# Encoder layer: a plain half chunk behind the Strassen products, a written VectorE order, and x loaded again for the folded input

## The chip, the cores and the metric

The kernel runs on one core of one Trainium2 chip. The metric is the device time of one execution in microseconds; the median of several executions counts.

## The reference

All tensors are float32; the sequence has 1,024 positions, the model 1,024 columns.

```python
def reference(x, pre_g, post_g, w_in, ln_g, ln_b, w_s, b_s, w_f, b_f, w_out):
    h = rms_norm(x, pre_g)
    p = jnp.einsum('bsd,de->bse', h, w_in)
    u_a, v_a, g_a, z_b, g_b = jnp.split(p, 5, axis=-1)       # 512 columns each
    a = spatial_gating(gelu(u_a), gelu(v_a), w_s, b_s, ln_g, ln_b) * silu(g_a)
    b = fourier_mix(z_b, w_f, b_f) * silu(g_b)               # real part of a 2D DFT, then w_f
    y = jnp.einsum('bse,ed->bsd', jnp.concatenate([a, b], axis=-1), w_out)
    return x + rms_norm(y, post_g)
```

## The kernel before, in words

Every product is made in parts: an operand is split into a high part (fp32r, made by ScalarE in `split`, L71) and a low part (what is left, made by VectorE, L74), and `mm3` (L76) issues high times high, high times low and low times high. So a product of 128x128 by 128x512 is three instructions on TensorE, and nothing can be multiplied until ScalarE and VectorE have both handled it.

The program has four stages. **Start** (L82 to L156): eight blocks of x, transposed (`head` and `xr`), come in with the columns of `w_in` for v; ScalarE makes `hh`, VectorE `hl`, both scaled by `pre_g`, and TensorE starts with v for seven chunks of 128 positions. `vec_sb` holds `pre_g` and other vectors; `const_load` (L254) brings `w_f` and the tables, but the table `cs_sb` is loaded early on SP. **Features** (L423, `feature_tile`): twelve tiles of 128 features, each in two halves of 512 positions; the epilogue frees the bank `pf` with the VectorE operation `t<-pf,R` (L474, L481). Between them the function `after` (L493) places the other work by tables: the folded input of z (`z_fold`, L298, for eight blocks), the products with it (`z_step`), the gating heads and the DFTs. `z_fold` adds `hh` and `hl`, multiplies by `R` (the norm of each position), adds and subtracts mirrored positions into `sd`, and splits that into `fh` and `fl`. `feature_load` (L260) loads one tile's weights `wf` and splits them, `wz_load` (L225) loads z's weights and folds them into `fw`.

**Out projection** (L610 on). Eight chunks of 128 positions; chunk c has two halves n of 512 output columns. Chunks 0 and 1 are made plainly: four half chunks of two products each (L704), bank `py`. Chunks 2 to 7 are made in pairs g = 1, 2, 3 by seven Strassen products each, `q1` to `q7` and `p2` (a product is twelve instructions of 512 columns). Their weights are quarters of `w_out` (`11`, `12`, `21`, `22`) and sums of them, `T1` to `T4` (`w_sum`, L549): one part is added by VectorE, or by a load that accumulates on POOL's queue (L554), and the result is split again (`w_split`). `stream` (L687) makes the operands `cq` one step ahead. The results are combined on VectorE out of the banks `ba`, `bb`, `bc` into `y` (L744 to L775); `bb` is used by `q6`, then by `q7` and `q4`. `ORDER` (L601) runs group 1 by itself and interleaves groups 2 and 3; the last group's `q1` and `p2` are cut in two halves of 256 columns. `y_part` (L642) takes the sum of squares of a part: ScalarE squares, VectorE adds into `part`; `y_out` scales and stores: chunks below `DIRECT` (6) are scaled on VectorE (L667), get x by an accumulating load and go out; 6 and 7 have x loaded ahead.

All tiles of 4 KB a partition share 40 buffers (tag `S`); a tile waits for the last reader of its buffer. TensorE's order is the written one throughout; VectorE's is the written one from L729 on (`tc.manual_schedule`), and elsewhere, as on ScalarE, POOL and SP, a scheduler of the framework sets it when the program is built.

Of the kernel before, what the change touches and what calls it, by code (L numbers as in the profile page):

```python
# [8 lines left out]
F32 = mybir.dt.float32  # L9
# [5 lines left out]
P = 128  # L15
# [16 lines left out]
def encoder_layer_kernel(  # L32
# [48 lines left out]

    head = slot("head")  # L82
    wv0 = raw_slot("wv0")
    vec_sb = con.tile([P, 20], F32, name="vec_sb")
    nc.scalar.dma_start(vec_sb, x0[:, 0:20])
    nc.sync.dma_start(head[:, 0:256], x0[:, 20:276])
    nc.sync.dma_start(wv0[:, 0:512], w_nat[1, 0])
    nc.sync.dma_start(head[:, 256:1024], x0[:, 276:1044])
    pre_g, ln_g, b_f, ln_b = (vec_sb[:, a:b] for a, b in ((0, 8), (8, 12), (12, 16), (16, 20)))
# [28 lines left out]

    def square(kt):
        if kt == 0:  # L120
            nc.scalar.activation(sq, xs[kt], AF.Square)
        else:
            sq1 = tmp(f"sq{kt}")
            nc.scalar.activation(sq1, xs[kt], AF.Square)
            nc.vector.tensor_tensor(sq, sq, sq1, op=ALU.add)

    wvh = quad("wvh", (P, 8, 512), F32R)
    for kt in range(KT):
        if kt == 0:
# [12 lines left out]
        h = slot(f"hh{kt}", dt=F32R)  # L142
        l = slot(f"hl{kt}", dt=F32R)
        hh.append(h)
        hl.append(l)
        if kt == 0:
            split(wrv, wh, wl, hi_on_act=False)
        for sl in ([slice(0, 256), slice(256, 640), slice(640, 1024)] if kt == 0 else [slice(0, 1024)]):
            nc.scalar.activation(h[:, sl], xr[:, sl], AF.Copy, scale=pg)  # L149
            nc.vector.scalar_tensor_tensor(l[:, sl], xr[:, sl], pg, h[:, sl].bitcast(F32), op0=ALU.mult, op1=ALU.subtract)  # L150
        if kt > 0:
            split(wrv, wh, wl)
        if kt > 0:
            square(kt - 1)
        xs[kt] = xr
# [92 lines left out]

    wsTb = slot("wsTb", (P, 2, 512))
    ws_sb, Tb = wsTb[:, 0], wsTb[:, 1]  # L250
    cs_sb = con.tile([P, 129], F32, name="cs_sb")
    wf_sb = slot("wf_sb", (P, 512))

    def const_load():  # L254
        nc.sync.dma_start(ws_sb, w_sT)
# [41 lines left out]

    def z_fold(kt):  # L298
        hs = tmp(f"hs{kt}")
        nc.vector.tensor_tensor(hs, hh[kt].bitcast(F32), hl[kt].bitcast(F32), op=ALU.add)  # L300
        nc.vector.tensor_tensor(hs, hs, R, op=ALU.mult)
        sd = tmp(f"sd{kt}", (P, 2, 4, P))
        hv = hs.rearrange("p (b a) -> p a b", a=8)
        for i, op in enumerate((ALU.add, ALU.subtract)):
# [112 lines left out]

    wss = slot("wss", (P, 2, 512), F32R)
    split(ws_sb, wss[:, 0], wss[:, 1])
    wq.append(feature_load(1))  # L420


    def feature_tile(f, epilogue):  # L423
# [125 lines left out]
    def w_sum(key, i, base, add):  # L549
        t = raw.pop((base, i))  # L550
        if (add, i) in raw:
            nc.vector.tensor_tensor(t, t, raw[add, i], op=ALU.add)  # L552
        else:
            nc.gpsimd.dma_start(t, quarter(add, i), accum_op=ALU.add)  # L554
        raw[key, i] = t
        w_split(key, i, t)

    mixB = lambda: Bf[0]

# [38 lines left out]
        yield  # L598

    FULL = ("q1", "q5", "q6", "p2", "q7", "q3", "q4")  # L600
    ORDER = [(1, k) for k in FULL] + [(2, k) for k in ("q1", "q5", "q6", "q3", "q7")] + [(3, k) for k in FULL[:3]]  # L601
    ORDER += [(2, "q4"), (3, "q7"), (2, "p2")] + [(3, k) for k in ("q4", "q3", "p2")]
    WITH = {"q1": "11", "q5": "T1", "q6": "T2", "p2": "21", "q7": "T3", "q3": "22", "q4": "T4"}

    def product(o, t, key, start, stop, lo=0, hi=512):
# [4 lines left out]
    for f in range(8, 12):  # L610
        feature_tile(f, g_epilogue(lambda f=f: Bf[0][:, f - 8]))
        if f < 10:
            w_load(("11", "21")[f % 2], 0)
            del raw[("11", "21")[f % 2], 0]
        elif f == 10:
            for key in ("11", "21"):
                w_load(key, 1)
                del raw[key, 1]
        if f == 11:
            for key in ("12", "22"):  # L620
                for i in range(2):
                    w_raw(key, i)

    x_t = x.rearrange("(c p) d -> c p d", c=8)
    out_t = out.rearrange("(c p) d -> c p d", c=8)
    xin, yt, ssq, part = {}, {}, {}, {}
    pg_sb = slot("pg_sb")

    DIRECT = 6

    def x_load(c):
        if c < DIRECT:
            return
        xin[c] = slot(f"x{c}")
        nc.sync.dma_start(xin[c], x_t[c])
# [6 lines left out]
    def y_part(c, n, src, lo, hi, outs=()):  # L642
# [13 lines left out]
        if c >= DIRECT:  # L656
            nc.vector.tensor_tensor(yt[c][:, lo:hi], src, pg_sb[:, lo:hi], op=ALU.mult)  # L657
        if j == n - 1:
            if outs:
# [2 lines left out]
                due.append(c)  # L662

    def y_out(c, outs):
        if c < DIRECT:
            for src, lo, hi in ready[c]:
                nc.vector.scalar_tensor_tensor(yt[c][:, lo:hi], src, part[c], pg_sb[:, lo:hi], op0=ALU.mult, op1=ALU.mult)  # L667
            nc.gpsimd.dma_start(yt[c], x_t[c], accum_op=ALU.add)
        for lo, hi in outs:
            if c >= DIRECT:  # L670
# [6 lines left out]
    for key in ("12", "22"):  # L677
        for i in range(2):
            w_split(key, i, raw[key, i])
    for i in range(2):  # L680
        w_raw("11", i)
    nc.sync.dma_start(pg_sb, post_g.broadcast_to([P, D]))
# [4 lines left out]
    def stream():  # L687
        old = None
        for g, key in ORDER:
# [4 lines left out]
            old = o  # L694
            yield
        next(old)
        yield

    ahead = stream()
    def make_sum(j):  # L700
        for i in range(2):
            w_sum(sums[j][0], i, *sums[j][1:])

    for k in range(4):  # L704
        n, c = k // 2, k % 2
        if n == 0:
            yt[c] = slot(f"y{c}")
        py = bank(f"py{c}{n}")
        product(py, pl[c][0], "1" + str(n + 1), True, False)
        product(py, pl[c][1], "2" + str(n + 1), False, True)  # L710
        make_sum(k)
        next(ahead)
        if k == 1:
            for i in range(2):
                raw.pop(("22", i))
        if k > 1:
            next(ahead)
            x_load(c)
        y_part(c, 2, py, n * 512, n * 512 + 512, [(0, D)])

    lo, hi = slice(0, 512), slice(512, 1024)
    def y_due(cs):
        for c in list(cs):
            if c in due:
                due.remove(c)
                y_out(c, [(0, D)])

    at = {}
    ctx.enter_context(tc.manual_schedule(engines={mybir.EngineType.DVE}))  # L729
    for g, key in ORDER:  # L730
        a, b = 2 * g, 2 * g + 1
        last = g == 3
        op = ops.pop((g, key))
        before = due[:]
        if key == "q1":
            at[g] = [bank(f"b{n}{g}") for n in ("abcd" if last else "abc")]
            yt[a], yt[b] = slot(f"y{a}"), slot(f"y{b}")
        ba, bb, bc = at[g][:3]
        if key == "q1" and last:
            for t, (l, h) in zip((ba, at[g][3]), cuts):  # L740
                product(t[:, 0:256], op, "11", True, False, l, h)
                nc.scalar.copy(yt[b][:, l:h], t[:, 0:256])
        elif key == "q1":
            product(ba, op, "11", True, False)  # L744
            nc.scalar.copy(yt[b][:, lo], ba)
        elif key == "q5":
# [2 lines left out]
        elif key == "q6":  # L749
            product(bb, op, "T2", True, False)  # L750
            nc.vector.tensor_tensor(yt[a][:, hi], bb, yt[b][:, lo], op=ALU.subtract)
            x_load(b)
        elif key == "q7":
            product(bb, op, "T3", False, False)
            nc.vector.tensor_tensor(yt[b][:, hi], bb, yt[b][:, hi], op=ALU.add)
            y_part(b, 2, yt[b][:, hi], 512, 1024)
            x_load(a)
        elif key == "q4":
            product(bb, op, "T4", False, True)
            nc.vector.tensor_tensor(yt[b][:, lo], yt[b][:, lo], bb, op=ALU.subtract)  # L760
            y_part(b, 2, yt[b][:, lo], 0, 512)
        elif key == "q3":
            product(bc, op, "22", False, True)
            nc.vector.tensor_tensor(yt[a][:, hi], bc, yt[a][:, hi], op=ALU.add)  # L764
            if last:
                y_due(before)
            y_part(a, 3 if last else 2, yt[a][:, hi], 512, 1024)
        elif last:
            for t, (l, h) in zip((ba, at[g][3]), cuts):
                product(t[:, 0:256], op, "21", False, True, l, h)  # L770
                y_part(a, 3, t[:, 0:256], l, h, [(512, 1024), (0, 512)])
        else:
            product(ba, op, "21", False, True)
            y_part(a, 2, ba, 0, 512)
        y_due(before)  # L775
        next(ahead, None)
        if (g, key) == (2, "p2"):
            y_due(due)


def _dft_consts():
# [49 lines left out]
```

## Time and profile before

| what | value |
|---|---|
| median of 3 executions (lowest, highest) | 320.06 us (319.32, 320.10) |
| the profiled execution | 321.24 us |
| its span (first to last instruction) | 319.5 us |
| granted clock of TensorE, mean | 0.991 of full speed |
| busy: TensorE, VectorE, ScalarE, GpSimd | 96%, 78%, 42%, 8% |

The span is what the trace covers; the 1.7 us that the profiled execution takes beyond it are outside the program's instructions. The list of waits says for each engine what it waited for, by the instruction that released it. The timeline gives start and length of single instructions; the lengths of matrix products overlap, so the distance between two starts is what one costs.

### The profile page before, as it was taken

What the parts mean: (1) busy time and instruction counts of PE and PEld (TensorE: products, weight loads), DVE (VectorE), ACT (ScalarE), POOL (GpSimd) and SP (SyncE); (2) the same over time, 40 slices, a digit from 0 to 9 for tenths busy, and PEclk for the clock granted to TensorE, in tenths of its full rate; (3) what the DMA queues carried; (4) which work ended last, traced back from release to release, by engine and by line L of the source; (5) the groups of instructions that cost most, each with busy time, mean ns of one, the idle gap of its engine ahead of it and who ended that gap; (6) DMA issues with size and microseconds to landing.
All of it is one profiled execution on the core that took longest, in us unless ns stands there. A gap on an engine that the chain in (4) does not pass through costs nothing. (4 is left out here: it accounts for less than half of the span.)

```text
span 319.5 us, 4048 instructions
## 1 busy us (share of the span) xinstructions
PE 307.3 (96%) x1513; PEld 256.8 (80%) x1513; DVE 247.9 (78%) x465; ACT 134.0 (42%) x211; POOL 25.0 (8%) x35
## 2 busy tenths in 40 slices
PE   8999999999999999899999999999999999999990
PEld 7688888878888888788888888888888878888880
DVE  4599399899899899889746889663899887865562
ACT  4794467830311313342342343531746454333220
POOL 0000033200000000000000000000013420300140
PEclk9999999999999999999999999999999999999996
DMA  7984102021011120102010116730507855284067
GB/s 246 409 308 135 63 0 68 1 75 58 0 67 68 40 91 2 50 0 96 37 66 2 67 51 220 205 117 2 197 0 132 133 133 131 34 230 131 0 121 276
DMA packets 12548, 32.46 MB, mean 102 GB/s; under 512 B 1264, under 2 KB 1520, under 8 KB 12528
## 3 DMA queue, kind: packets, MB, share of 16 engines
q1 hardware_dynamic: 10432, 26.95, 24.1%
q0 software_dynamic: 1952, 5.24, 9.5%
q8 instruction: 12, 0.20, 0.2%
q14 instruction: 8, 0.07, 0.1%
q10 hardware_dynamic: 144, 0.01, 0.0%
HBM read 28.00 MB, written 4.19 MB: 101 GB/s over the span
## 5 line engine op out<-in xcount | busy, mean ns | idle before, releaser
L71 ACT CAST fh<-sd 128x1024 fp32r<-128x1024 f32 x8 | 8.4, 1049 | 41.3 <-DVE sd L307 35.6
L79 PE MATMUL pv<-wvh,hl 128*128 128x512 f32 x57 | 22.6, 396 | 0.6 <-DVE hl L150 0.6
L77 PE MATMUL pv<-wvh,hh 128*128 128x512 f32 x57 | 22.6, 396 | 0.0
L78 PE MATMUL pv<-wvl,hh 128*128 128x512 f32 x57 | 22.5, 394 | 0.0
L481 DVE TENSOR_TENSOR t<-pf,R 128x512 f32<-128x512 f32 x16 | 11.0, 685 | 13.3 <-PE pf L79 13.2
L482 ACT ACTIVATE t<-t 128x512 f32<-128x512 f32 x16 | 10.1, 630 | 26.1 <-DVE t L481 26.0
L554 POOL DMA_DIRECT2D wo<-in_w_out x4 | 5.1, 1384 | 185.0 <-DVE wo L552 179.7
L319 PE MATMUL pz<-wzh,fh 128*128 128x260 f32 x64 | 18.0, 282 | 0.0
L319 PE MATMUL pz<-wzl,fh 128*128 128x260 f32 x64 | 18.0, 281 | 0.0
L319 PE MATMUL pz<-wzh,fl 128*128 128x260 f32 x64 | 18.0, 281 | 0.0
L305 DVE TENSOR_TENSOR sd<-hs 128x384 f32<-128x384 f32 x16 | 14.6, 913 | 0.2
L595 ACT CAST cq<-s 128x512 fp32r<-128x512 f32 x12 | 7.3, 620 | 17.2 <-DVE s L587 17.2
L74 DVE TENSOR_TENSOR fl<-sd,fh 128x1024 fp32r<-128x1024 f32 x8 | 9.8, 1224 | 5.5 <-ACT fh L71 5.5
L79 PEld LDWEIGHTS pv<-wvh,hl 128*128 128x128 f32 x57 | 10.7, 188 | 3.5 <-DVE hl L150 1.0
L77 PEld LDWEIGHTS pv<-wvh,hh 128*128 128x128 f32 x57 | 10.7, 188 | 2.9 <-ACT hh L149 0.4
L78 PEld LDWEIGHTS pv<-wvl,hh 128*128 128x128 f32 x57 | 10.7, 188 | 2.5
L319 PEld LDWEIGHTS pz<-wzl,fh 128*128 128x128 f32 x64 | 12.1, 189 | 0.3
L319 PEld LDWEIGHTS pz<-wzh,fh 128*128 128x128 f32 x64 | 12.0, 188 | 0.3
L319 PEld LDWEIGHTS pz<-wzh,fl 128*128 128x128 f32 x64 | 12.1, 189 | 0.0
L150 DVE SCALAR_TENSOR_TENSOR hl<-xr,vec_sb,hh 128x1024 fp32r<-128x1024 f32 x7 | 9.0, 1279 | 3.4 <-ACT hh L149 3.4
L650 ACT ACTIVATE jk<-y 128x512 f32<-128x512 f32 x9 | 5.7, 631 | 12.9 <-DVE y L760 7.2
L475 ACT ACTIVATE mixA<-t 128x512 f32<-128x512 f32 x8 | 5.0, 631 | 13.4 <-DVE t L474 13.3
(455 smaller groups left out, 980.3 us busy)
## 6 DMA issues: line engine op xcount, KB each, us to landing
wo<-in_w_out SPq DMA_DIRECT2D x10, 512.0 KB, 4.6
xr<-in_xT SPq DMA_DIRECT2D x7, 512.0 KB, 7.6
out<-y SPq DMA_DIRECT2D x7, 512.0 KB, 3.5
y<-in_x POOLq DMA_DIRECT2D x6, 512.0 KB, 5.2
wv<-in_w_nat SPq DMA_DIRECT2D x8, 256.0 KB, 7.7
wz<-in_w_nat SPq DMA_DIRECT2D x4, 512.0 KB, 4.0
wo<-in_w_out POOLq DMA_DIRECT2D x4, 512.0 KB, 7.2
x<-in_x SPq DMA_DIRECT2D x2, 512.0 KB, 4.0
```

The lines of the kernel that those rows point to most:

```text
L71: nc.scalar.copy(hi, src)
L74: nc.vector.tensor_tensor(lo, src, hi.bitcast(F32), op=ALU.subtract)
L77: nc.tensor.matmul(o, lh, rh, start=start, stop=False, **kw)
L78: nc.tensor.matmul(o, lh, rl, start=False, stop=False, **kw)
L79: nc.tensor.matmul(o, ll, rh, start=False, stop=stop, **kw)
L150: nc.vector.scalar_tensor_tensor(l[:, sl], xr[:, sl], pg, h[:, sl].bitcast(F32), op0=ALU.mult, op1=ALU.subtract)
L305: nc.vector.tensor_tensor(sd[:, i, 1:4], hv[:, 1:4], hv[:, 7:4:-1, ::-1], op=op)
L319: nc.tensor.matmul(pz[t][:, cs], l[:, i, t], r[:, cs], start=kt == 0 and i == 0 and j == 0, stop=kt == KT - 1 and i == 1 and j == 2, skip_ ...
L481: nc.vector.tensor_tensor(t, pf, R[:, sl], op=ALU.mult)
L482: nc.scalar.activation(t, t, AF.Silu)
L595: nc.scalar.copy(t[:, 0], src)
L650: nc.scalar.activation(jk[:, 0:w], src, AF.Square, accum_out=ssq[c][:, j:j + 1])
```

## The change

Six edits. (1) At the start `vec_sb` and the first 256 columns of x are one load into one tile `head0`; `cs_sb` is loaded with `w_f`, into the same buffer. (2) `feature_load(1)` stands ahead of `wz_load(1)`. (3) `z_fold` loads its block of x again (eight loads on SP) and makes `(x * pre_g) * R` in one VectorE operation where there were two. (4) In the out projection the loads and splits of `w_out` are placed earlier, and the sums `T1` to `T4` are split apart from being made, `T3` and `T4` by a table `LATE`. (5) VectorE's order is the written one from the first plain half chunk on, and the combination of a product stands where the loop writes it. (6) `ORDER` runs three groups one after the other with whole products; the plain half chunk of chunk 1's first 512 columns is made last, cut in two halves of 256; `DIRECT` is chunks 1, 6 and 7.

```diff
-    vec_sb = con.tile([P, 20], F32, name="vec_sb")
-    nc.scalar.dma_start(vec_sb, x0[:, 0:20])
-    nc.sync.dma_start(head[:, 0:256], x0[:, 20:276])
+    head0 = con.tile([P, 276], F32, name="head0")
+    vec_sb = head0[:, 0:20]
+    nc.sync.dma_start(head0, x0[:, 0:276])
...
-            nc.scalar.activation(sq, xs[kt], AF.Square)
+            nc.scalar.activation(sq[:, 0:256], head0[:, 20:276], AF.Square)
+            nc.scalar.activation(sq[:, 256:1024], head[:, 256:1024], AF.Square)
...
-    cs_sb = con.tile([P, 129], F32, name="cs_sb")
-    wf_sb = slot("wf_sb", (P, 512))
+    wfcs = slot("wfcs")
+    wf_sb, cs_sb = wfcs[:, 0:512], wfcs[:, 512:641]
...
             const_load()
+            wq.append(feature_load(1))
             wz_load(1)
...
-        nc.vector.tensor_tensor(hs, hh[kt].bitcast(F32), hl[kt].bitcast(F32), op=ALU.add)
-        nc.vector.tensor_tensor(hs, hs, R, op=ALU.mult)
+        nc.sync.dma_start(hs, xT[kt - 1] if kt else x0[:, 20:1044])
+        nc.vector.scalar_tensor_tensor(hs, hs, pre_g[:, kt:kt + 1], R, op0=ALU.mult, op1=ALU.mult)
...
-    ORDER = [(1, k) for k in FULL] + [(2, k) for k in ("q1", "q5", "q6", "q3", "q7")] + [(3, k) for k in FULL[:3]]
-    ORDER += [(2, "q4"), (3, "q7"), (2, "p2")] + [(3, k) for k in ("q4", "q3", "p2")]
+    ORDER = [(g, k) for g in range(1, 4) for k in FULL]
...
-    DIRECT = 6
+    DIRECT = 1, 6, 7
...
+        pl[1] = plain_ops(1)
...
+    ctx.enter_context(tc.manual_schedule(engines={mybir.EngineType.DVE}))
+    for k, (c, n) in enumerate(((0, 0), (0, 1), (1, 1))):
...
+    LATE = {"q1": (2, 0), "q5": (2, 1), "q6": (3, 0), "p2": (3, 1)}
...
+        if g > 1 or key in FULL[4:]:
+            y_due(before)
+        if g == 1 and key in LATE:
+            j, i = LATE[key]
+            w_low(sums[j][0], i)
+            if key == "q5":
+                w_high("T4")
+        if (g, key) == (3, "q7"):
+            x_load(1)
+            yt[1] = slot("y1")
+            y_part(1, 3, pys[1, 1], 512, 1024)
+    y_due(due)
+    for l, h in cuts:
+        py = bank(f"py1{l}")[:, 0:256]
+        product(py, pl[1][0], "11", True, False, l, h)
+        product(py, pl[1][1], "21", False, True, l, h)
+        y_part(1, 3, py, l, h, [(512, 1024), (0, 512)])
```

SP's queue at the start, before (`head` and `xr` are blocks of x, `wv` weights of v):

```order
L86 DMA head<-in_x 128x256
L87 DMA wv_68<-in_w_nat 128x512
L88 DMA head<-in_x 128x768
L141 DMA wv_68<-in_w_nat 128x512
L257 DMA cs_sb<-in_dft 128x129
L133 DMA xr_111<-in_xT 128x1024
L133 DMA xr_121<-in_xT 128x1024
```

and now (`head_69` is the tile `head0`):

```order
L86 DMA head_69<-in_x 128x276
L87 DMA wv_68<-in_w_nat 128x512
L88 DMA head<-in_x 128x768
L142 DMA wv_68<-in_w_nat 128x512
L134 DMA xr_110<-in_xT 128x1024
L134 DMA xr_121<-in_xT 128x1024
```

The load of `cs_sb`, which stood ahead of the second block of x, is gone from here, and the first load is 20 columns wider.

VectorE at `wf5l` (the low half of feature tile 5's weights) and fold 5, before:

```order
L74 TENSOR_TENSOR wf5l<-wf5r,wf5h 128x1024
L300 TENSOR_TENSOR hs_1078<-hh_164,hl_165 128x1024
L301 TENSOR_TENSOR hs_1078<-hs_1078,R 128x1024
L305 TENSOR_TENSOR sd_1081<-hs_1078 128x384
L306 TENSOR_TENSOR sd_1081<-hs_1078 128x127
L307 COPY sd_1081<-hs_1078 128x1
L305 TENSOR_TENSOR sd_1081<-hs_1078 128x384
L306 TENSOR_TENSOR sd_1081<-hs_1078 128x127
L307 COPY sd_1081<-hs_1078 128x1
L74 TENSOR_TENSOR fl_1089<-sd_1081,fh_1088 128x1024
L481 TENSOR_TENSOR t<-pf_1116,R 128x512
```

and now:

```order
L74 TENSOR_TENSOR wf5l<-wf5r,wf5h 128x1024
L483 TENSOR_TENSOR t<-pf_1115,R 128x512
L304 SCALAR_TENSOR_TENSOR hs_1077<-hs_1077,head_69,R 128x1024
L470 SCALAR_TENSOR_TENSOR gate<-pg_1158,head_69,wsTb 128x512
L308 TENSOR_TENSOR sd_1080<-hs_1077 128x384
L309 TENSOR_TENSOR sd_1080<-hs_1077 128x127
L310 COPY sd_1080<-hs_1077 128x1
L308 TENSOR_TENSOR sd_1080<-hs_1077 128x384
L309 TENSOR_TENSOR sd_1080<-hs_1077 128x127
L310 COPY sd_1080<-hs_1077 128x1
```

The epilogue `t<-pf` stood behind the whole fold and now stands ahead of it; the fold starts with one operation on the loaded `hs`.

VectorE in the first Strassen group, around the combination of `q6` (`y<-bb`), before (`py` is a plain half chunk, `wo…l` a low half of a sum):

```order
L667 SCALAR_TENSOR_TENSOR y_2077<-py_2166,rsy,pg_sb 128x512
L74 TENSOR_TENSOR woT40l<-wo_2071,woT40h 128x1024
L74 TENSOR_TENSOR woT41l<-wo_2073,woT41h 128x1024
L597 TENSOR_TENSOR cp_2207<-mixB,cp_2207 128x512
L597 TENSOR_TENSOR cq_2254<-s_2255,cq_2254 128x512
L651 TENSOR_SCALAR part<-ssq,part 128x1
L597 TENSOR_TENSOR cq_2259<-s_2260,cq_2259 128x512
L667 SCALAR_TENSOR_TENSOR y_2120<-py_2121,rsy,pg_sb 128x512
L667 SCALAR_TENSOR_TENSOR y_2120<-py_2218,rsy,pg_sb 128x512
L748 TENSOR_TENSOR y_2278<-bc_2276,y_2278 128x512
L593 SCALAR_TENSOR_TENSOR cq_2293<-mixB,cq_2293 128x512
L751 TENSOR_TENSOR y_2277<-bb_2275,y_2278 128x512
```

and now:

```order
L548 TENSOR_TENSOR woT30l<-wo_1975,woT30h 128x1024
L761 TENSOR_TENSOR y_2210<-bc_2208,y_2210 128x512
L607 TENSOR_TENSOR cp_2225<-mixB,cp_2225 128x512
L597 TENSOR_TENSOR s_2243<-mixA 128x512
L548 TENSOR_TENSOR woT31l<-wo_1977,woT31h 128x1024
L764 TENSOR_TENSOR y_2209<-bb_2207,y_2210 128x512
L607 TENSOR_TENSOR cq_2242<-s_2243,cq_2242 128x512
L597 TENSOR_TENSOR s_2268<-mixB,s_2197 128x512
L548 TENSOR_TENSOR woT40l<-wo_2070,woT40h 128x1024
L607 TENSOR_TENSOR cq_2267<-s_2268,cq_2267 128x512
L659 TENSOR_SCALAR part<-ssq 128x1
```

Before, both halves of `T4`, scalings of plain chunks (L667) and operands of later products stood ahead of `y<-bb`; now only `T3` and the next operands do.

## Rows read from the trace of the kernel before

**Rows 1.** The page, busy time of each engine, its share and its instructions.

```profile
PE 307.3 (96%) x1513; PEld 256.8 (80%) x1513; DVE 247.9 (78%) x465; ACT 134.0 (42%) x211; POOL 25.0 (8%) x35
```

**Rows 2.** The waits of TensorE: us in total, times, longest.

```profile
PE pf L77 <- DVE t L481: 1.0, 1, 1.0
PE pv L79 <- DVE hl L150: 0.6, 1, 0.6
PE bb L77 <- DVE y L751: 0.5, 1, 0.5
PE pf L79 <- DVE wf1l L74: 0.4, 1, 0.4
```

**Rows 3.** Timeline of TensorE: start, length, instruction, idle time before and releaser.

```profile
262.63 0.40 PE L79 MATMUL ba<-wo211h,cp 128*128 128x512 f32 x1
263.54 0.50 PE L77 MATMUL bb<-woT30h,cq 128*128 128x512 f32 x1 [0.51 <-DVE y L751]
263.88 0.40 PE L78 MATMUL bb<-woT30l,cq 128*128 128x512 f32 x1
```

**Rows 4.** Timeline of TensorE: first plain product, two Strassen products, last instruction.

```profile
229.56 0.39 PE L77 MATMUL py<-wo110h,pla 128*128 128x512 f32 x1
...
272.00 0.40 PE L77 MATMUL ba<-wo110h,cq 128*128 128x512 f32 x1
...
274.76 0.40 PE L77 MATMUL bc<-woT10h,cq 128*128 128x512 f32 x1
...
310.80 0.28 PE L79 MATMUL bd<-wo211h,cp 128*128 128x256 f32 x1
```

**Rows 5.** Timeline of SP, ScalarE and VectorE at the start.

```profile
2.59 0.44 SPq L257 DMA_DIRECT2D cs_sb<-in_dft  x1
...
9.69 1.15 ACT L149 ACTIVATE hh<-xr,vec_sb 128x1024 fp32r<-128x1024 f32 x1 [2.50 <-DMA xr<-in_xT]
...
10.88 1.28 DVE L150 SCALAR_TENSOR_TENSOR hl<-xr,vec_sb,hh 128x1024 fp32r<-128x1024 f32 x1 [2.85 <-ACT hh L149]
```

**Rows 6.** Timeline of VectorE around the second tile of feature weights.

```profile
58.45 0.68 DVE L234 TENSOR_TENSOR fw<-wz 128x504 f32<-128x504 f32 x1
...
63.36 1.22 DVE L74 TENSOR_TENSOR wf1l<-wf1r,wf1h 128x1024 fp32r<-128x1024 f32 x1
```

**Rows 7.** Timeline around fold 5: VectorE, then TensorE.

```profile
122.40 1.22 DVE L74 TENSOR_TENSOR wf5l<-wf5r,wf5h 128x1024 fp32r<-128x1024 f32 x1
123.53 1.22 DVE L300 TENSOR_TENSOR hs<-hh,hl 128x1024 f32<-128x1024 f32 x1
...
131.68 0.47 PE L77 MATMUL pf<-hh,wf5h 128*128 128x512 f32 x1 [0.96 <-DVE t L481]
```

**Rows 8.** The page, DMA issues: times, KB each, us to landing.

```profile
wz<-in_w_nat SPq DMA_DIRECT2D x4, 512.0 KB, 4.0
```

**Rows 9.** Timeline of ScalarE and VectorE in the first Strassen group.

```profile
255.58 1.05 ACT L71 CAST woT41h<-wo 128x1024 fp32r<-128x1024 f32 x1 [1.94 <-DMA wo<-in_w_out]
...
260.28 1.41 DVE L667 SCALAR_TENSOR_TENSOR y<-py,rsy,pg_sb 128x512 f32<-128x512 f32 x2 [0.47 <-POOL rsy L103]
...
262.80 0.68 DVE L751 TENSOR_TENSOR y<-bb,y 128x512 f32<-128x512 f32 x1
```

**Rows 10.** Timeline of ScalarE and VectorE after the last product.

```profile
311.45 0.19 ACT L650 ACTIVATION_READ_ACCUMULATOR jk<-bd 128x1 f32 x1
...
311.87 0.20 DVE L651 TENSOR_SCALAR part<-ssq,part 128x1 f32<-128x1 f32 x1
```

**Rows 11.** DMA issues from 314.25, from 262 to 268, and below 1 us.

```profile
out<-y SPq DMA_DIRECT2D x1, 256.0 KB, 3.5
...
out<-y SPq DMA_DIRECT2D x1, 512.0 KB, 2.6
...
head<-in_x SPq DMA_DIRECT2D x1, 128.0 KB, 2.3
```

**Rows 12.** The waits of VectorE, the line for ScalarE's sums of squares.

```profile
DVE part L651 <- ACT jk L650: 8.1, 9, 1.4
```

More of the change, by code (lines that the diff above doesn't have):

```diff
@@ L148, in encoder_layer_kernel @@
         for sl in ([slice(0, 256), slice(256, 640), slice(640, 1024)] if kt == 0 else [slice(0, 1024)]):
-            nc.scalar.activation(h[:, sl], xr[:, sl], AF.Copy, scale=pg)
-            nc.vector.scalar_tensor_tensor(l[:, sl], xr[:, sl], pg, h[:, sl].bitcast(F32), op0=ALU.mult, op1=ALU.subtract)
+            src = head0[:, 20:276] if kt == 0 and sl.start == 0 else xr[:, sl]
+            nc.scalar.activation(h[:, sl], src, AF.Copy, scale=pg)
+            nc.vector.scalar_tensor_tensor(l[:, sl], src, pg, h[:, sl].bitcast(F32), op0=ALU.mult, op1=ALU.subtract)
         if kt > 0:
@@ L419, in encoder_layer_kernel @@
     split(ws_sb, wss[:, 0], wss[:, 1])
-    wq.append(feature_load(1))
     def feature_tile(f, epilogue):
@@ L537, in encoder_layer_kernel, with w_high, w_low @@
     raw = {}
+    def w_high(key):
+        for i in range(2):
+            W[key, i] = slot(f"wo{key}{i}h", (P, 2, 512), F32R), slot(f"wo{key}{i}l", (P, 2, 512), F32R)
+            nc.scalar.copy(W[key, i][0], raw[key, i])
+    def w_low(key, i):
+        h, l = W[key, i]
+        nc.vector.tensor_tensor(l, raw[key, i], h.bitcast(F32), op=ALU.subtract)
     def w_raw(key, i):
@@ L555, in w_sum @@
         raw[key, i] = t
-        w_split(key, i, t)
     mixB = lambda: Bf[0]
@@ L612, in encoder_layer_kernel @@
         if f < 10:
-            w_load(("11", "21")[f % 2], 0)
-            del raw[("11", "21")[f % 2], 0]
+            for key in ("11", "21"):
+                w_load(key, f - 8)
+                del raw[key, f - 8]
         elif f == 10:
[L616 to L619, printed above, removed]
             for key in ("12", "22"):
@@ L622, in encoder_layer_kernel @@
                     w_raw(key, i)
+            for i in range(2):
+                w_split("12", i, raw["12", i])
     x_t = x.rearrange("(c p) d -> c p d", c=8)
@@ L627, in encoder_layer_kernel @@
     pg_sb = slot("pg_sb")
-    DIRECT = 6
+    DIRECT = 1, 6, 7
     def x_load(c):
-        if c < DIRECT:
+        if c not in DIRECT:
             return
@@ L655, in y_part @@
             part[c] = rs
-        if c >= DIRECT:
+        if c in DIRECT:
             nc.vector.tensor_tensor(yt[c][:, lo:hi], src, pg_sb[:, lo:hi], op=ALU.mult)
@@ L664, in y_out @@
     def y_out(c, outs):
-        if c < DIRECT:
+        if c not in DIRECT:
             for src, lo, hi in ready[c]:
@@ L669, in y_out @@
         for lo, hi in outs:
-            if c >= DIRECT:
+            if c in DIRECT:
                 nc.vector.scalar_tensor_tensor(yt[c][:, lo:hi], yt[c][:, lo:hi], part[c], xin[c][:, lo:hi], op0=ALU.mult, op1=ALU.add)
@@ L676, in encoder_layer_kernel @@
     pl = [plain_ops(c) for c in range(2)]
-    for key in ("12", "22"):
-        for i in range(2):
-            w_split(key, i, raw[key, i])
+    for i in range(2):
+        w_split("22", i, raw["22", i])
     for i in range(2):
@@ L696, in stream @@
         next(old)
+        pl[1] = plain_ops(1)
         yield
[L699 to L721, printed above, removed]
     def y_due(cs):
@@ L726, in y_due, with make_sum, split_sum @@
                 y_out(c, [(0, D)])
+    ahead = stream()
+    def make_sum(j):
+        for i in range(2):
+            w_sum(sums[j][0], i, *sums[j][1:])
+    def split_sum(j):
+        for i in range(2):
+            w_split(sums[j][0], i, raw[sums[j][0], i])
+    ctx.enter_context(tc.manual_schedule(engines={mybir.EngineType.DVE}))
+    pys = {}
+    for k, (c, n) in enumerate(((0, 0), (0, 1), (1, 1))):
+        if n == 0:
+            yt[c] = slot(f"y{c}")
+        py = pys[c, n] = bank(f"py{c}{n}")
+        product(py, pl[c][0], "1" + str(n + 1), True, False)
+        product(py, pl[c][1], "2" + str(n + 1), False, True)
+        next(ahead)
+        if k < 2:
+            make_sum(k)
+            split_sum(k)
+        if k == 1:
+            for i in range(2):
+                raw.pop(("22", i))
+            make_sum(2)
+            make_sum(3)
+        if c == 0:
+            y_part(c, 2, py, n * 512, n * 512 + 512)
+    lo, hi = slice(0, 512), slice(512, 1024)
     at = {}
-    ctx.enter_context(tc.manual_schedule(engines={mybir.EngineType.DVE}))
+    w_high("T3")
+    LATE = {"q1": (2, 0), "q5": (2, 1), "q6": (3, 0), "p2": (3, 1)}
     for g, key in ORDER:
         a, b = 2 * g, 2 * g + 1
-        last = g == 3
         op = ops.pop((g, key))
@@ L735, in encoder_layer_kernel @@
         if key == "q1":
-            at[g] = [bank(f"b{n}{g}") for n in ("abcd" if last else "abc")]
+            at[g] = [bank(f"b{n}{g}") for n in "abc"]
             yt[a], yt[b] = slot(f"y{a}"), slot(f"y{b}")
[L738 to L743, printed above, removed]
+        ba, bb, bc = at[g]
+        done = None
+        if key == "q1":
             product(ba, op, "11", True, False)
@@ L752, in encoder_layer_kernel @@
             x_load(b)
+        elif key == "p2":
+            product(ba, op, "21", False, True)
+            done = a, ba, 0, 512
         elif key == "q7":
@@ L755, in encoder_layer_kernel @@
             nc.vector.tensor_tensor(yt[b][:, hi], bb, yt[b][:, hi], op=ALU.add)
-            y_part(b, 2, yt[b][:, hi], 512, 1024)
+            done = b, yt[b][:, hi], 512, 1024
             x_load(a)
[L758 to L761, printed above, removed]
         elif key == "q3":
@@ L764, in encoder_layer_kernel @@
             nc.vector.tensor_tensor(yt[a][:, hi], bc, yt[a][:, hi], op=ALU.add)
[L765 to L771, printed above, removed]
-        else:
-            product(ba, op, "21", False, True)
-            y_part(a, 2, ba, 0, 512)
-        y_due(before)
+            done = a, yt[a][:, hi], 512, 1024
+        else:
+            product(bb, op, "T4", False, True)
+            nc.vector.tensor_tensor(yt[b][:, lo], yt[b][:, lo], bb, op=ALU.subtract)
+            done = b, yt[b][:, lo], 0, 512
         next(ahead, None)
-        if (g, key) == (2, "p2"):
-            y_due(due)
+        if done:
+            y_part(done[0], 2, *done[1:])
+        if g > 1 or key in FULL[4:]:
[15 more added lines that the diff above has]
+        y_part(1, 3, py, l, h, [(512, 1024), (0, 512)])
 def _dft_consts():
```

## The prediction

> **What bounds the kernel now.** I read the page's busy shares first: TensorE works in 307.3 of 319.5 us [rows 1], so nothing can be won but its idle time and what lies after its last product. The list of what TensorE waited for names four places inside the kernel, each a single wait for VectorE: 0.6 us for `hl` at the start, 0.4 for `wf1l`, 1.0 for `t` (a PSUM bank that the epilogue frees) and 0.5 for a combination `y` that frees bank `bb` [rows 2]. The timeline tells what one of them costs. In [rows 3] the last product before the wait starts at 262.63 and the next at 263.54, where neighbours start 0.23 apart: 0.68 lost, and the first product after the wait is itself slow (0.34 to the next), another 0.11. So a wait of 0.51 in the list cost 0.79, 0.28 more than listed. With the same addition the four are worth about 0.87, 0.66, 1.20 and 0.79 us. The last product starts at 310.80 [rows 4] and the span ends at 319.5; those 8.7 us of tail are the fifth place.
>
> **What the change leaves alone.** TensorE has as many instructions as before, and as many narrow ones: the 256-wide halves of the last group's `q1` and `p2` (48 products) are now whole, and the two operands of the moved plain chunk (48 products) are cut instead. Three plain half chunks of 5.5 us stand ahead of the Strassen loop, not four, and the fourth stands behind it. One Strassen product takes 2.76 us (272.00 to 274.76 in [rows 4]), before and after. Nothing is gained by the move itself.
>
> **Start.** The 64.5 KB load of `cs_sb` no longer stands ahead of the second block of x on SP. It held SP for 0.44 us [rows 5], and that block (issued behind it) is what ScalarE waited for until 9.69, and VectorE's `hl`, and so TensorE. The tiny `vec_sb` load on ScalarE's queue goes into the first load of x. Bounds: nothing, if the DMA engines were the limit and not the issue; 0.48 us, if the block lands earlier by the whole slot on SP. I take 0.3, as the DMA engines were busy too and only 64.5 KB of some 1,600 KB ahead are gone. The squares of the first block become two ScalarE instructions; they stand behind `hh`, and no wait of TensorE is for them.
>
> **`wf1l`.** Its low half is made at 63.36, behind a fold of `wz` that starts at 58.45 [rows 6]. The load now stands ahead of that `wz`, and so do its two splits, by the order of VectorE. The low half then ends near 59.7, 4 us before TensorE asks. Gain 0.66; bound below, nothing, if another late piece takes its place.
>
> **Folds.** Each of eight `z_fold` calls had two VectorE operations of 1.22 us and now has one. It is a scalar_tensor_tensor of 1,024 columns; that form took 1.28 [rows 5] where the plain one took 1.22 [rows 7]. That saves 1.16 each, 9.3 us of VectorE in all, none of it on the path except through what stands behind a fold. In [rows 7] `wf5l` starts at 122.40, fold 5 follows, and TensorE goes on at 131.68 after 0.96 of waiting for the `t` behind it. In the new order `t` stands between `wf5l` and fold 5 and can start near 123.6, 7 us before it is needed. Gain 1.20, bound below nothing. Its price is eight 512 KB loads on SP. They enter a slot that must be free, so each waits for an earlier reader; a load of that size from the same queue took 4.0 [rows 8]. By the two orders a slot is read for the last time well ahead of the fold that waits for it; the least cover is there for fold 7, whose slot is freed by the last product of a feature half, behind the load of the DFT tables. If its load is late VectorE waits there, a whole feature half (48 products) ahead of TensorE's use.
>
> **Strassen stage.** In [rows 9] ScalarE got the second half of T4 only at 255.58, the low halves and scalings of plain chunks stood ahead of the combination on VectorE, and `bb` was freed at 263.48. In the written order the combination of `q6` stands ahead of both T4 halves and of all scalings. I walk the new order with durations from the rows, TensorE entering group 1 near 246.2 (229.56 in [rows 4] and six times 2.76): `q6` ends at 254.6, VectorE has by then done T3's first half (to 251.0), two operands and T3's second half (to 255.0), frees `bb` at 255.7, and `q7` asks for it at 257.3. Cover 1.6 us; gain 0.79. The next tight places are the low half of `q3`'s operand (259.5, needed at 260.6) and of group 2's `q1` (265.1, needed at 266.1). VectorE's load in group 1 is 7 operands, 4 differences, 5 combinations at 0.68, 2 scalings at 0.70, 4 T halves at 1.22 and 4 sums at 0.2: 18.0 of the 19.3 us that seven products take; groups 2 and 3 have no T halves and two scalings more, 14.5. No later wait is gone or added, but the cover is about 1 us throughout group 1.
>
> **Tail.** Two terms. VectorE's last sum started at 311.87 although ScalarE had read its accumulator by 311.64 [rows 10], because two other chunks were being finished. Now chunk 7 is ready 2.7 us after `q4` ends and its and chunk 6's last scalings (1.28 each, the form of [rows 5]) are done 0.6 us before TensorE stops, so the sum follows at once: gain 0.2. Second, the last two stores of 256 KB took 3.5 us to land, behind 512 KB stores still in flight, where a 512 KB store alone took 2.6 and a 128 KB load at the start 2.3 [rows 11]. Now stores 6 and 7 are issued some 2 and 0.7 us before TensorE stops and the last two 2.3 and 3.0 us after, on empty queues. I take 2.5, nearest to the store alone: gain 1.0, between 0.8 (2.7) and 1.2 (2.3).
>
> The Trainium skill ("DMA: Bandwidth & Descriptors", section on the anatomy of one DMA) fits a transfer as 2.0 us plus its bytes at 436 GB/s. By that a 256 KB store lands in 2.6 us and the sum would be 0.1 us smaller; its 3.2 for 512 KB is above the 2.6 of the row, so the row is taken.
>
> **Sum.** 0.3 + 0.66 + 1.20 + 0.79 + 0.2 + 1.0 = 4.15 us. The profiled execution took 321.24 us with a span of 319.5; it would come to about 317.1. The median of the runs shown is 320.06, 1.2 below that execution; the same difference gives **315.9**.
>
> **Rivals.**
> *Only the last stage gains.* The loads of x come late or VectorE's new order in the first 140 us puts another operand behind a fold, so waits of the same size (2.2 us) stand elsewhere. For it: these orders come from a scheduler that knows no landing times. Against: it has 9.3 us less to do. The time is 320.06 - 2.0 = 318.1.
> *The written order gives part back.* ScalarE's sums of squares stand in VectorE's order ahead of operands; VectorE waited up to 1.4 us for one of those before [rows 12]. If two such waits in group 1 exceed its cover of 1 us, TensorE loses about 1 us each, 2 to 3 in all: 318 to 319. Against: in the walk other work stands between.
> *Slower: T4 holds both orders.* ScalarE casts T4's second half when its accumulating load lands, and in its order the sum of `p2` and `q3`'s operand stand behind. From landing to that operand it takes 1.05 for the cast [rows 9], half of that and 0.19 [rows 10] for the sum, half for the operand, 2.3 us; TensorE asks at 260.1, so a landing after 257.8 costs its whole delay. The cast began at 255.58, and the sum is made at the same time as before. It is slower than before only from 261.8 on, 6 us late; at 263 the time is 321.
> *A queue of loads.* SP takes loads in order, so a fold's load that waits for its slot holds the weight load behind it. `wf5l` is made 8 us before TensorE reads it [rows 7], and the slot of each fold's load is freed ahead of the slot of the weights behind it; a hold past 8 us would be a loss, 6 us past it would give 322. The Trainium skill (same page and section) says that a semaphore wait happens on the issuing sequencer before dispatch. By that rule such a hold is real; the trace bears out only that SP itself waited.
> That the change does not do what it says is excluded by the orders shown above.
>
> **Numbers.** Forecast 0.60; last stage only 0.18; part given back 0.12; T4 0.06; queue of loads 0.04. A measurement of this kernel can tell 0.3% (1 us) from no change. Faster is the forecast, the second case and half of the third: 0.84; same is the other half of the third: 0.06; slower 0.10. The forecast's own range is 314.9 to 317.0, by the bounds of start and tail and one of the 0.66 and 1.20 missing. To hold 8 in 10 the range takes in the second case: 314.7 to 318.4.
>
> **What would show it.** Right: in the list of TensorE's waits, `wf1l`, `t` and `y` are gone, `hl` is below 0.4, and no new line is above 0.3; the last products start near 308; the last two stores land in 2.3 to 2.7 us. Wrong: a TensorE wait for an operand `cq` or for `bb` in group 1, a VectorE wait for a load of `hs` above 1 us with a TensorE wait behind it, or last stores that still take 3.5.

## The result, and the profile after

The changed kernel takes **314.99 us** in the median (314.79 to 315.11, 4 runs) against 320.00 (319.32 to 320.10, 4 runs): a ratio of 0.9847, 95% interval 0.983 to 0.9864, so it is 4.9 us faster, between 4.4 and 5.4. The forecast was 315.9 us, a gain of 4.15.

The page's busy line after, which answers to [rows 1]:

```profile
PE 305.6 (98%) x1513; PEld 257.1 (82%) x1513; DVE 241.7 (77%) x460; ACT 134.7 (43%) x213; POOL 22.4 (7%) x34
```

The list of what TensorE waited for (total us, times, longest), which answers to [rows 2], is one line, at the program's start (the list of before has it too, with the same 1.1):

```profile
PE warm L111 <- DVE ones L92: 1.1, 1, 1.1
```

All four waits of [rows 2] are gone and none has come. VectorE's longest wait for a sum of squares, which answers to [rows 12], is shorter as well:

```profile
DVE part L659 <- ACT jk L658: 3.6, 7, 0.9
```

The clock has no part in the gain: in both profiles the granted clock is 1.00 of full speed (the level of 2.4 GHz) in every stretch up to the last product, and 0.50 (1.2 GHz) only in the tail, where TensorE has nothing left to do. The means of 0.991 and 0.995 differ by that stretch.

The timeline of TensorE where `q7` begins (start, length, instruction; compare [rows 3]) and at its last instruction (compare [rows 4]):

```profile
253.46 0.39 PE L79 MATMUL ba<-wo211h,cp 128*128 128x512 f32 x1
253.69 0.39 PE L77 MATMUL bb<-woT30h,cq 128*128 128x512 f32 x1
253.91 0.39 PE L78 MATMUL bb<-woT30l,cq 128*128 128x512 f32 x1
...
306.34 0.28 PE L79 MATMUL py<-wo211h,plb 128*128 128x256 f32 x1
```

VectorE's timeline at the places of [rows 6, 7, 9] and in the tail:

```profile
57.21 1.23 DVE L74 TENSOR_TENSOR wf1l<-wf1r,wf1h 128x1024 fp32r<-128x1024 f32 x1 [0.39 <-ACT wf1h L71]
...
118.38 1.22 DVE L74 TENSOR_TENSOR wf5l<-wf5r,wf5h 128x1024 fp32r<-128x1024 f32 x1
119.52 0.69 DVE L483 TENSOR_TENSOR t<-pf,R 128x512 f32<-128x512 f32 x1
120.12 1.28 DVE L304 SCALAR_TENSOR_TENSOR hs<-hs,head,R 128x1024 f32<-128x1024 f32 x1
...
251.37 0.69 DVE L764 TENSOR_TENSOR y<-bb,y 128x512 f32<-128x512 f32 x1
...
307.23 0.21 DVE L659 TENSOR_SCALAR part<-ssq,part 128x1 f32<-128x1 f32 x1 [0.58 <-ACT jk L658]
...
308.16 1.41 DVE L679 SCALAR_TENSOR_TENSOR y<-y,rsy,x 128x512 f32<-128x512 f32 x2 [0.39 <-POOL rsy L103]
```

`bb` is free at 252.06 and asked for at 253.69, a cover of 1.6 us. The DMA issues of the tail (one window each; times, KB, us to landing; compare [rows 11]), and on the page the new loads of x:

```profile
out<-y SPq DMA_DIRECT2D x1, 256.0 KB, 2.1
...
out<-y SPq DMA_DIRECT2D x1, 256.0 KB, 2.0
...
hs<-in_xT SPq DMA_DIRECT2D x7, 512.0 KB, 3.3
```

Where the time went between the two profiles: the span fell by 6.4 us, the last product starts 4.46 earlier (310.80 and 306.34), and from there to the end of the span it is 6.76 us and not 8.7. That is more than the medians give, because the profiled execution of the kernel before (321.24) had a slow start, as a second one shows below. Against that second one the last product is 2.65 earlier and the tail (from the start of the last product to the end of the span) 1.95 shorter. The second one, at 319.45, is the fastest of its eleven executions (median 320.18), so a usual execution of the kernel before lies between the two.

### The profile page after: what moved, and what is told of

It reads as the page before. It is cut to its first block, busy times and chain, and to the rows that moved or that the text cites. A ratio compares the mean times of both kernels' runs of the same rounds, so it can differ in the third digit from the quotient of the medians.

```text
span 313.1 us, 4049 instructions
## 1 busy us (share of the span) xinstructions
PE 305.6 (98%) x1513; PEld 257.1 (82%) x1513; DVE 241.7 (77%) x460; ACT 134.7 (43%) x213; POOL 22.4 (7%) x34
## 4 chain that ended last, share of the span: by engine, by line
PE 98%; DVE 0%; DVEq 0%; POOLq 0%; ACT 0%; issue 0%; ACTq 0%
PE pf L77 14%; PE pf L79 14%; PE pf L78 14%; PE pz L322 7%; PE pv L79 4%; PE pv L78 4%; PE pv L77 4%; PE bb L77 3%; PE bb L78 3%; PE bb L79 3%; PE py L79 2%; PE py L77 2%; PE py L78 2%; PE pg L468 2%; PE ba L77 2%; PE bc L79 2%
## 5 line engine op out<-in xcount | busy, mean ns | idle before, releaser
L607 DVE TENSOR_TENSOR cq<-s,cq 128x512 fp32r<-128x512 f32 x12 | 8.2, 687 | 2.8 <-ACT cq L605 2.8
```

The source lines that it names most:

```text
L607: nc.vector.tensor_tensor(t[:, 1], src, t[:, 0].bitcast(F32), op=ALU.subtract)
```

## The experiments

Each kernel ran beside the kernel before on the same chip; the ratio is to those runs. Differences from the changed kernel's 314.99 are between runs on different chips, on which the kernel before gave medians of 319.94 to 320.25.

| kernel | median us | before us | ratio, 95% interval |
|---|---|---|---|
| before again | 320.18 | 320.25 | 0.9998 (0.9986 to 1.0011) |
| before + start | 320.26 | 320.25 | 1.0006 (0.9993 to 1.0019) |
| before + `cs_sb` later | 320.64 | 320.25 | 1.0014 (1.0004 to 1.0024) |
| before + fold | 318.51 | 319.94 | 0.9952 (0.9939 to 0.9964) |
| before + early load + fold | 318.09 | 320.19 | 0.9932 (0.9918 to 0.9947) |
| last stage alone | 317.31 | 320.19 | 0.9909 (0.9897 to 0.9922) |
| changed, start of before | 315.35 | 319.94 | 0.9859 (0.9846 to 0.9872) |
| changed, late load | 317.22 | 319.96 | 0.9910 (0.9896 to 0.9923) |
| changed, old fold | 317.54 | 320.19 | 0.9921 (0.9908 to 0.9933) |
| changed, two operations a fold | 315.81 | 319.96 | 0.9872 (0.9858 to 0.9886) |
| changed, all plain chunks in front | 317.05 | 320.19 | 0.9902 (0.9889 to 0.9916) |
| changed, first load on ScalarE's queue, 6 warming products | 315.24 | 319.96 | 0.9863 (0.9839 to 0.9887) |

### The start

Before again, unchanged.

> The kernel before, once more, for a second profiled execution. The profiled spans differ by 6.4 us (319.5 and 313.1) where the medians differ by 5.0. If the first profile of before was an outlier by some 1.2 us, this one has a span near 318.2 and the missing 1.2 us lie either at the start (the second block's hh begins near 8.5 and not at 9.69) or in the tail (last stores land in some 2.5 us and not 3.5). If profiles of before are like that as a rule, the span is 319.3 to 319.6 and the difference lies in the time that is outside the span.

The span is 317.7 us in an execution of 319.45. TensorE's waits:

```profile
PE pf L77 <- DVE t L481: 1.0, 1, 1.0
PE pf L79 <- DVE wf1l L74: 0.4, 1, 0.4
PE pv L79 <- DVE hl L150: 0.3, 1, 0.3
```

ScalarE began the second block's `hh` earlier than in [rows 5]:

```profile
8.32 1.15 ACT L149 ACTIVATE hh<-xr,vec_sb 128x1024 fp32r<-128x1024 f32 x1 [1.01 <-DMA xr<-in_xT]
```

So the same program has its second block 1.4 us earlier or later (8.32 and 9.69), its first product of v at 4.49 or 5.11, and the wait for `bb` may be missing from the list (a gap of 0.25 is left there). `wf1l` and `t` stand in both, at the same size. Of the 1.8 us between the two spans 1.4 lay ahead of the first row sum (the products that sum the squares of x; 34.86 and 36.24) and 0.4 at `bb`; the tail was the same, 8.7. The 9.69 is the far end: in the four other profiles that have the old start the second block's `hh` begins at 8.15 to 8.93.

Before with the start alone, edit (1) of the diff.

> The kernel before with the start of the change alone (vec_sb in the first load of x, cs_sb loaded with w_f). Term of the prediction: 0.3 us, at most 0.5, so 319.5 to 320.0. By the two profiles the whole of 1.7 us comes from here (v's first block starts 0.61 earlier, the wait for hl is gone), so 318.3. Rival, the landing of loads differs from execution to execution: 320.0, with hh of the second block anywhere between 8 and 9.7.

It changes nothing (320.26), and before with `cs_sb` later alone is no faster either:

```diff
-    cs_sb = con.tile([P, 129], F32, name="cs_sb")
-    wf_sb = slot("wf_sb", (P, 512))
+    wfcs = slot("wfcs")
+    wf_sb, cs_sb = wfcs[:, 0:512], wfcs[:, 512:641]
```

> Before with only cs_sb loaded later. If SP's slot is what counts: the second block's hh begins 0.4 to 0.5 earlier than in before, TensorE's first product of v does not move (5.1), the time falls by 0.3 to 0.5. If the DMA engines' time for its 128 short packets counts too: hh begins 1 us earlier or more, the time falls by 0.6 to 1.0.

It is 0.4 us slower (320.64; the interval of its ratio is all above 1). The second block's `hh` begins at 8.27 and the first product of v at 4.50, both as in the second profile of before, and TensorE's wait for `wf1l` is 1.5 us. Before with only `vec_sb` merged gave no result, as its tiles do not fit: the pool `sm` needs 9.5 KB a partition and 9.03 were left. So the two halves of edit (1) are not told apart.

The list of waits of before with the start alone shows where time was lost again:

```profile
PE pf L79 <- DVE wf1l L74: 1.4, 1, 1.4
PE bb L77 <- DVE y L753: 0.5, 1, 0.5
PE pf L77 <- DVE t L483: 0.5, 1, 0.5
PE pv L79 <- DVE hl L152: 0.3, 1, 0.3
```

The wait for `wf1l` went from 0.4 to 1.4. VectorE's timeline of that kernel at 62.7:

```profile
62.73 0.69 DVE L476 TENSOR_TENSOR t<-pf,R 128x512 f32<-128x512 f32 x1 [0.53 <-PE pf L79]
63.34 1.22 DVE L74 TENSOR_TENSOR wf1l<-wf1r,wf1h 128x1024 fp32r<-128x1024 f32 x1
```

The scheduler now had an epilogue of tile 0 ahead of `wf1l`; VectorE idled 0.53 us for TensorE, and TensorE then waited for VectorE. A change in the loads had moved another engine's order. By the timelines the stretch with `wf1l` is 1.09 us longer than in the second profile of before and the one with `t` 0.46 shorter, so the edit adds about 0.6 us there. If the median still doesn't change, the start itself gains about as much; that is worked out, not shown.

The changed kernel with the start of before (edit (1) undone).

> The changed kernel with the start of before (vec_sb by its own load, cs_sb early on SP). In the kernel before the new start gave nothing in the median, but there VectorE's order had an epilogue ahead of wf1l and TensorE waited 1.4 us for it. Here wf1l stands early in both. If the new start is worth its 0.3 us: 315.3. If its loads only scatter less: 315.0 to 315.1 with a wider spread. If the early landing counts fully (1.4 us in the first profile of before): 316 or more.

It takes 315.35 us against 314.99, 0.36 more, with a wait for `hl` of 0.2; the intervals overlap, so 0.3 us is plausible and not shown. The changed kernel with its first load on the other queue and two warming products less, so two edits at once:

```diff
-    nc.sync.dma_start(head0, x0[:, 0:276])
+    nc.scalar.dma_start(head0, x0[:, 0:276])
...
-WARM = 8
+WARM = 6
```

> The changed kernel with its first load of x on ScalarE's queue, beside the load of wv on SP, and 6 warming products instead of 8. TensorE waits for nothing after 4.49 us in the changed kernel, so an earlier first product is the only gain left at the start. If wv lands 0.4 earlier (issued at 0.74 and not 1.17): first product of v near 4.0, 314.6. If TensorE's clock is granted later for it: the first products are slower by as much, 315.0. If the landing times scatter as they do in the runs of before (first product 4.49 to 5.11): no clear difference.

No gain (315.24). From ScalarE's and TensorE's timeline:

```profile
3.88 0.51 ACT L151 ACTIVATE hh<-head 128x256 fp32r<-128x256 f32 x1 [1.12 <-DMA head<-in_x]
...
4.43 1.22 PE L274 MATMUL pv<-wvh,hh 128*128 128x512 f32 x2 [0.45 <-ACT hh L151]
```

The two loads, both issued at 0.74, landed nearly together: `wv` 0.2 us earlier than in the changed kernel (VectorE cast it at 3.70, not 3.89), x 0.9 later (3.88, not 2.94). The first product waited for x instead of running behind the warming products, and its runs scatter more (314.63 to 317.08).

### `wf1l` and the folds

Before with the fold alone, edit (3).

> Before with the new fold alone, the second feature tile still loaded late. In VectorE's order wf1l stands behind the wz fold as before (wait of 0.4 stays), t stands behind fold 5's first operation only. By the term of the prediction: 1.2 less, 319.0 beside 320.2, no wait for t. If the new loads of x delay other loads on SP: 319.5 to 320.5 with a wait for a weight tile. With the 318.1 of both edits together the rest, 0.7 to 0.9, is then wf1l.

It is 1.4 us faster; its interval, 1.15 to 1.95, just takes in the 1.2. The wait for `t` is gone, that for `wf1l` stays at 0.4. Before with the early load and the fold, edits (2) and (3).

> Before with the early load of the second feature tile and the new fold, nothing else. By the sum: 0.66 for wf1l and 1.2 for t, so 318.3 beside 320.2; TensorE keeps its waits for hl and for bb and has none for wf1l and t. Rival, the gains of the parts don't add because a wait that is removed hands its time to the next: 319.3 or more, with a new or longer wait between 70 and 262 us.

It is 2.1 us faster. The waits left are 0.6 for the first `hh`, 0.2 for `hl` and 0.2 for `bb`. In TensorE's timelines of this kernel and of the second profile of before the way from the first row sum to the first gating product, in which `wf1l` lies, is 33.41 and 34.08 us, the one from tile 4 to tile 5 is 15.75 and 16.83: gains of 0.67 and 1.08 for terms of 0.66 and 1.20. The share of `wf1l` rests on the timelines: this kernel's median is only 0.4 us below the one with the fold alone, and the intervals of the two ratios overlap.

The changed kernel with the late load, edit (2) undone.

> The changed kernel with the load of the second feature tile behind the second wz again. By the term of the prediction: 0.66 more, 315.7, with a wait for wf1l of 0.4. As in the kernels with the start alone the order of VectorE has an epilogue ahead of wf1l, and the wait was 1.4 there: 1.7 more, 316.7, unless a later wait takes less for it, and the changed kernel has none to give back. In its order fold 5's first operation stands ahead of t, no wait expected there, since VectorE is some 5 us ahead.

It is 2.2 us slower than the changed kernel, over three times the term. The one wait behind the start, which no other takes over:

```profile
PE pf L79 <- DVE wf1l L74: 1.4, 1, 1.4
```

VectorE's order has the epilogue ahead of `wf1l` again. By the timelines this stretch (first row sum to first gating product) is 1.72 us longer than in the changed kernel; in the profiled execution another 0.6 lies ahead of the first row sum, where `wv` landed late (first product at 5.00).

The changed kernel with the old fold, edit (3) undone:

```diff
-        nc.sync.dma_start(hs, xT[kt - 1] if kt else x0[:, 20:1044])
-        nc.vector.scalar_tensor_tensor(hs, hs, pre_g[:, kt:kt + 1], R, op0=ALU.mult, op1=ALU.mult)
+        nc.vector.tensor_tensor(hs, hh[kt].bitcast(F32), hl[kt].bitcast(F32), op=ALU.add)
+        nc.vector.tensor_tensor(hs, hs, R, op=ALU.mult)
```

> The changed kernel with the fold of before (hh plus hl, two operations, no second load of x). In its order t stands behind the adds and mirrors of fold 5 but ahead of its low half fl. If t's place ahead of the fold is worth 1.1 us as the prediction has it: 315.5 to 316.1 with a wait for t of some 0.3 to 0.9. If the order alone counts and this place is early enough: 315.0. If VectorE's 9.3 us more of work tell elsewhere: above 316.5 with several waits.

It takes 317.54 us, 2.55 more than the changed kernel and above what was expected of a place. Its waits:

```profile
PE pf L77 <- DVE t L483: 0.9, 1, 0.9
PE pf L77 <- DVE t L476: 0.6, 1, 0.6
PE pv L79 <- DVE hl L152: 0.5, 1, 0.5
```

and VectorE there:

```profile
123.84 1.22 DVE L74 TENSOR_TENSOR wf5l<-wf5r,wf5h 128x1024 fp32r<-128x1024 f32 x1
...
129.86 0.68 DVE L483 TENSOR_TENSOR t<-pf,R 128x512 f32<-128x512 f32 x1
```

The two waits for `t` lie between tile 4 and tile 5, a stretch that is 1.96 us longer than in the changed kernel; the rest, 0.6, lies ahead of the first row sum. Two readings are open here: `t` stands behind the adds and mirrors of fold 5, and VectorE comes to `wf5l` 5.5 us later than in the changed kernel (0.6 of it from its start). The next kernel tells them apart:

```diff
-        nc.vector.scalar_tensor_tensor(hs, hs, pre_g[:, kt:kt + 1], R, op0=ALU.mult, op1=ALU.mult)
+        nc.vector.tensor_scalar_mul(hs, hs, pre_g[:, kt:kt + 1])
+        nc.vector.tensor_tensor(hs, hs, R, op=ALU.mult)
```

> The changed kernel with the second load of x, but two operations in each fold (times pre_g, 0.7 us by the row of pg_sb, then times R, 1.22): 5 us more work on VectorE than the changed kernel, 4.6 less than with the old fold. In its order t stands ahead of wf5l and fold 5. If t's place is what counts (the prediction): no wait for t, 315.0. If VectorE's amount of work up to there counts (with the old fold it came to wf5l 4.9 us later and TensorE waited twice, 317.5): about half of that comes back, 316.0 to 316.5.

It takes 315.81 us. VectorE comes to `wf5l` later still (125.24), but one `t` stands ahead of it and the next right behind:

```profile
121.53 0.69 DVE L484 TENSOR_TENSOR t<-pf,R 128x512 f32<-128x512 f32 x1
125.24 1.23 DVE L74 TENSOR_TENSOR wf5l<-wf5r,wf5h 128x1024 fp32r<-128x1024 f32 x1
126.38 0.69 DVE L484 TENSOR_TENSOR t<-pf,R 128x512 f32<-128x512 f32 x1
```

and TensorE waits for no `t`:

```profile
PE pv L79 <- DVE hl L152: 0.4, 1, 0.4
PE pz L323 <- DVE fl L74: 0.3, 1, 0.3
```

So `t` in a place ahead of the fold is enough for TensorE not to wait, although VectorE is later, as the prediction had it. The added work costs 0.8 us here, of which 0.3 is a wait for a late fold. Place and work are not fully separated: the orders of the two kernels differ because the scheduler was given different work.

### The last stage

The last stage alone: edits (1) to (3) of the changed kernel undone.

> The changed kernel with start, early load and fold undone: the last stage alone. By the sum: 0.8 for bb and 1.2 for the tail, so 318.2; the second profile of before had no wait for bb, so the lower end of this is 319.0 and by the tail of the changed kernel's profile (last product to end of span 6.8 us against 8.7) 318.3. Waits for wf1l and t stay.

It is 2.9 us faster than before (2.5 to 3.3), for terms of 2.0. The tail is 6.7 us (last product 308.78, span 315.5), 2.0 less than in both profiles of before, and the list has no wait for `bb`:

```profile
PE pf L77 <- DVE t L481: 1.1, 1, 1.1
PE pf L79 <- DVE wf1l L74: 0.4, 1, 0.4
```

The changed kernel with the plain half chunk back in front:

```diff
-    for k, (c, n) in enumerate(((0, 0), (0, 1), (1, 1))):
+    for k, (c, n) in enumerate(((0, 0), (1, 0), (0, 1), (1, 1))):
...
-    DIRECT = 1, 6, 7
+    DIRECT = 6, 7
...
-        pl[1] = plain_ops(1)
...
+        if (g, key) == (3, "q4"):
+            y_due(before)
+            y_part(done[0], 2, *done[1:], [(512, 1024), (0, 512)])
```

(all four sums of squares follow their half chunk; the block at `q7` of group 3 and the loop behind the groups are gone).

> The changed kernel with all four plain half chunks ahead of the Strassen groups, so that q4 of group 3 is the last product, whole. By the sum the move itself gains nothing in TensorE's work, but the last chunk then needs a combination (0.68), a square over 512 and not 256 columns and two scalings after the last product: tail some 1.3 to 1.6 us longer, 316.4. Rival, the move matters for VectorE's cover in group 1 (four scalings of plain chunks come into group 1): also waits for bb or cq there, 317 or more. If the end is set by the stores alone: 315.3.

It takes 317.05 us, 2.1 more than the changed kernel, and TensorE waits for nothing behind the start in it either; group 1 bears the four scalings. Most of it is tail: from the last product, 306.74, to the end, 315.3, it is 8.56 us and not 6.76, so 1.8 more. The rest lies ahead of the first row sum, which comes 0.5 later in this execution. TensorE's last row and VectorE after it:

```profile
306.74 0.40 PE L79 MATMUL bb<-woT41h,cq 128*128 128x512 f32 x1
...
307.18 0.69 DVE L778 TENSOR_TENSOR y<-y,bb 128x512 f32<-128x512 f32 x1 [0.49 <-PE bb L79]
307.78 1.28 DVE L679 SCALAR_TENSOR_TENSOR y<-y,rsy,x 128x1024 f32<-128x1024 f32 x1
308.98 0.21 DVE L659 TENSOR_SCALAR part<-ssq,part 128x1 f32<-128x1 f32 x1
...
310.22 1.42 DVE L679 SCALAR_TENSOR_TENSOR y<-y,rsy,x 128x512 f32<-128x512 f32 x2 [0.44 <-POOL rsy L103]
```

From the last product's start to the last scalings it is 3.48 us here and 1.82 in the changed kernel; its last stores land in 2.0 as well. So with whole Strassen products at the end the chain is long and the queue empty; before, the chain was short (2.00 us, products cut in halves) and the queue full. The plain chunk at the end has both short.

## Why the prediction was right

- **Sign, mechanism and size.** 4.9 us against 4.15. All four waits named in the list are gone; the timelines show a gain for `wf1l`, `t` and `bb`, while that of the start is not shown beyond the noise. No rival came: VectorE's list of waits names no load of `hs`, `T4`'s second half did not hold `q4` or `q3`, and the written order has no wait in group 1 with the cover of 1.6 us that was walked.
- **The range and the signs.** The median lies 0.09 us above the lower end of the forecast's own range, and that is in part luck: the bounds named for the start (0.48) and the tail (1.2) give 315.5 at the least, and no term leads to the 314.9 that stands there. Two signs were missed. The last products were to start near 308 and do so at 306.34, as 310.80 had the slow start of that profile in it. The last stores were to land in 2.3 to 2.7 us and land in 2.0 and 2.1.
- **Start, 0.3.** 0.36 in the medians, not shown beyond the noise. In the first profile of before, against which the sum was made, the first row sum was 1.72 us behind the changed kernel's (36.24 and 34.52), since its loads had landed late; in the second it was 0.34 behind. So the first profile made the wait for `hl` look like a property of the program, and much of it was of the execution. Alone the edit gives nothing in the median, and the wait for `wf1l` grows.
- **`wf1l`, 0.66, and `t`, 1.20.** 0.67 and 1.08 by the timelines, 2.1 together by the runs. (The wait of 0.96 with the addition of 0.28 is 1.24, not 1.20.) Left out was that each depends on an order that the other edits set: undone in the changed kernel they cost 2.2 and 2.55 by the medians, 1.72 and 1.96 in their stretch of the timelines, and not 0.66 and 1.2, since the wait for `wf1l` is longer there and a second wait for `t` comes. The rival that only the last stage gains is excluded by the middle edits' own 2.1.
- **`bb`, 0.79.** It is 0.4 to 0.8: by the prediction's own count the wait cost 0.36 (0.25 and 0.11) in the second profile of before and 0.79 in the first. The cover that replaces it is as forecast.
- **Tail, 1.2: the step that was mis-sized.** It is 1.95 (8.7 to 6.76). The sum starts 0.18 earlier after the last product (term 0.2), but the stores land in 2.0 to 2.1 and not 2.5, so 1.5 instead of 1.0; the 2.6 of a 512 KB store was taken as nearest, and no row before showed a 256 KB store on an empty queue. The DMA engines were busy 96% of the time from 313 to 316 us in the kernel before and idle from 308.7 to 309.2 in the changed one. The fit that the prediction cites from the Trainium skill ("DMA: Bandwidth & Descriptors", section on the anatomy of one DMA) gives an estimate of 2.6 for such a store. The page states it for the path through GpSimd, and these stores are issued on SP; the measured 2.0 to 2.1 decides. The remaining 0.25 lies between the last scalings and the last store's landing. That nothing is gained by the move itself holds for TensorE's products; for the tail it is worth the 1.8 us by which the kernel with the chunk in front is longer there.

Sum by the runs: 0.36 + 2.1 + 2.9 = 5.4 against 4.9 (4.4 to 5.4) measured; the parts add up within that interval. No kernel tried beats the changed one.

## What to carry to other kernels

Where a scheduler orders an engine, an edit's price holds only in the company that it was measured in: look where each wait's releaser stands in the new order, and what stands ahead of it, rather than add up waits. When nothing stalls any more, end the program with the work whose result has the shortest way out, on an empty store queue. And take the start of one profile as one throw: a second profile of the same kernel tells which waits belong to the program.

## What was not expected of the hardware

A 256 KB store issued while the DMA engines were idle landed in 2.0 to 2.1 us, and in 3.5 behind stores of 512 KB. Two loads of 138 and 256 KB issued at once on two queues landed nearly together, the smaller one 0.9 us later than when it was issued 0.43 us ahead on the same queue as the other. The landing of the second block of x scatters by 1.4 us between executions of one program.
